# Matmuls on a tile of ones while the first loads run, the first norm's squares from the feature-major x, and first loads on two queues

## The chip, the cores and the metric

The kernel runs on one core of a Trainium2 chip. The metric is the device time of one execution in microseconds (us); the time before the change is the median of three runs. The core has a matrix engine (PE, with its weight loads shown apart as PEld), a vector engine (DVE), an activation engine (ACT), a general engine (POOL) and a queue engine (SP). Each works through its own list of instructions strictly in the order in which the program was built; an instruction that has to wait for another engine holds back everything behind it on its own engine. DMA transfers are issued from SP, ACT or POOL.

## The reference

One layer of a trunk on a sequence of 512 tokens with 1024 features, in float32:

```python
h = rms_norm(x, g[0])                      # x * rsqrt(mean(x^2) + eps) * g
y = hybrid_mixer(h, w_in, ...)             # four branches on proj = h @ w_in, gates on h @ w_gate
x = x + rms_norm(y, g[1])
h = rms_norm(x, g[2]); mem_n = rms_norm(mem, g[4])
x = x + rms_norm(cross_attention(h, mem_n, ...), g[3])
h = rms_norm(x, g[5])
x = x + rms_norm(conv_ffn(h, ...), g[6])
```

The change touches the first line alone, and the part of `proj` with which the kernel begins: the columns v (256, the values of the gated linear attention), a_lr (16, its decay input) and sv (256, the spatial gate's input).

## The kernel before

x is held feature-major, as eight tiles `x[k]` of 128 features by 512 tokens. A float32 product is made of three matmuls on operands split into a high and a low part (`hi`, `lo`): hi·hi, lo·hi and hi·lo. The norm's gain is folded into the split of x (`xgh`, `xgl`, lines 253 and 260), and its factor per token, rs0 = 1/sqrt(mean(x²) + eps), is applied only when a product leaves PSUM. So the matmuls can begin before the norm is known.

The first stage is a loop over the eight feature tiles k (lines 242 to 271). For each k it loads `x[k]` and a 128x528 slice of weights for v, a_lr and sv, splits both on ACT and DVE, and issues 18 matmuls: twelve of 272 columns into four banks `va` (one for each 128 tokens) and six of 256 columns into two banks `sv`. The sums of squares come from a second copy of x, token-major (`x_rows`): `RowNorm.step` loads 128x512 pieces, and ACT squares and sums each along its rows (`row`, lines 205 to 209), eight pieces in all. After the loop rs0 is one square root on ACT (line 194) and one reciprocal on DVE (line 195), and four small matmuls (`bctok`, line 221) spread it over the partitions into `rb0s`, so that it can also be applied to feature-major products.

Then the banks of the first stage are emptied by ACT with the factor rs0 (`svt`, `altok`, `vt`), the second half of the tokens of sv gets its 48 matmuls in the two banks that `svt` frees, `altok` is transposed on PE (`alT`), and the w_in products follow (`win`, 24 matmuls of 512 columns each, in the same two banks, tag A). Beside the first three w_in products runs the decay chain of the gated linear attention: matmuls `z`, then `ee` on ACT, which takes turns with the square root of the spatial gate's layer norm (`sd`, line 371) and with the constants of the recurrence (`la`, line 526), each needing another function table, then scans on DVE (line 421). `kr` (line 352) is the DVE instruction that empties the bank of each of the first two w_in products, and so lets the third and the fourth one start.

What sets the order on each engine is the building scheduler: it takes the instructions by priority and readiness by its own estimate and writes a fixed list for each engine; `with tc.high_priority()` (line 272) moves rs0 and `bctok` ahead as soon as it holds them for ready. The hardware then keeps to that list. SBUF slots (`get`, `put`) are reused in turn, and weights are loaded by SP two or three units ahead into four raw buffers, the same four that the first stage uses.

## Time and profile before

| | us |
|---|---|
| median of three runs (lowest, highest) | 963.23 (962.56, 964.26) |
| the profiled execution, its own time | 964.2 |
| its span in the trace | 960.8 |
| PE busy within the span | 944.7 |
| first matmul of the program, from the span's start | 4.52 |
| first matmul of the first w_in product | 31.97 |
| first matmul of the fourth w_in product | 54.49 |

The span is what the trace covers; 3.4 us of the execution's own time lie around it. Times of single rows are counted from the span's start. In a row of the timeline the first number is the start, the second the time until the end of the last of its instructions (x4 is four of them in a row), and brackets at its end name how long the engine had been idle and what released it. Matmuls are pipelined: the next one starts before the one ahead has ended, so the pace is read from start to start.

### The profile page before, as it was taken

How to read it: one execution, taken by the hardware profiler on the slowest of the kernel's cores; microseconds unless marked ns; L12 is line 12 of the kernel's file. 1: busy time of each engine (PE TensorE's matmuls, PEld its weight loads, DVE VectorE, ACT ScalarE, POOL GpSimd, SP SyncE). 2: the span in 40 equal slices, each digit the busy share in tenths (PEclk: the TensorE clock that was granted, in tenths of full speed). 3: DMA queues.
4: the chain of work that ended last, by engine and by line, in shares of the span. 5: the costliest groups of instructions: out<-in, count | busy, mean ns of one | idle time of the engine just before them, and what ended most of it. 6: DMA issues, size and time to landing. Idle time of an engine off the chain costs nothing.

```text
span 960.8 us, 12143 instructions
## 1 busy us (share of the span) xinstructions
PE 944.7 (98%) x4782; PEld 801.1 (83%) x4782; DVE 575.4 (60%) x886; ACT 420.8 (44%) x637; POOL 11.9 (1%) x33
## 2 busy tenths in 40 slices
PE   8999999999999999999999999999999999999996
PEld 8878887888888888899888899888888888888885
DVE  5876567535454567359854736887767777522414
ACT  7836336423232534356633645644444444322311
POOL 2000000000000000000000000000000000000001
PEclk9999999999999999999999999999999999999998
DMA  9432121232334332435322420232222323233302
GB/s 333 146 112 88 67 91 63 88 99 78 108 113 148 117 105 67 131 111 190 130 75 66 134 86 2 88 109 88 100 98 89 110 88 98 83 104 99 100 1 87
DMA packets 32648, 98.27 MB, mean 102 GB/s; under 512 B 4288, under 2 KB 7248, under 8 KB 32592
## 3 DMA queue, kind: packets, MB, share of 16 engines
q1 hardware_dynamic: 32416, 97.48, 31.2%
q8 instruction: 37, 0.61, 0.3%
q14 instruction: 19, 0.16, 0.0%
q0 software_dynamic: 32, 0.02, 0.0%
q10 hardware_dynamic: 144, 0.00, 0.0%
HBM read 95.39 MB, written 2.10 MB: 101 GB/s over the span
## 4 chain that ended last, share of the span: by engine, by line
PE 93%; DVE 2%; ACT 2%; issue 2%; DMA 0%; DVEq 0%; ACTq 0%
PE up L127 8%; PE up L126 8%; PE up L125 8%; PE gate L126 6%; PE gate L125 6%; PE gate L127 6%; PE dn L125 4%; PE dn L127 4%; PE dn L126 4%; PE win L125 3%; PE win L127 3%; PE win L126 3%; PE wo L125 2%; PE wo L127 2%; PE wo L126 2%
## 5 line engine op out<-in xcount | busy, mean ns | idle before, releaser
L75 ACT CAST whi<-raw 128x1024 fp32r<-128x1024 f32 x158 | 164.4, 1042 | 301.9 <-issue 142.0
L76 DVE TENSOR_TENSOR wlo<-raw,whi 128x1024 fp32r<-128x1024 f32 x158 | 191.3, 1213 | 130.1 <-ACT whi L75 128.8
L127 PE MATMUL up<-h3h,wlo 128*128 128x512 f32 (+1 forms) x368 | 138.2, 376 | 0.0
L126 PE MATMUL up<-h3l,whi 128*128 128x512 f32 (+1 forms) x368 | 138.1, 375 | 0.0
L125 PE MATMUL up<-h3h,whi 128*128 128x512 f32 (+1 forms) x368 | 138.1, 375 | 0.0
L125 PE MATMUL gate<-xgh,whi 128*128 128x512 f32 x256 | 99.8, 390 | 0.0
L126 PE MATMUL gate<-xgl,whi 128*128 128x512 f32 x256 | 99.7, 389 | 0.0
L127 PE MATMUL gate<-xgh,wlo 128*128 128x512 f32 x256 | 99.6, 389 | 0.0
L125 PEld LDWEIGHTS up<-h3h,whi 128*128 128x128 f32 x368 | 69.3, 188 | 12.6
L126 PEld LDWEIGHTS up<-h3l,whi 128*128 128x128 f32 x368 | 69.3, 188 | 12.4
L127 PEld LDWEIGHTS up<-h3h,wlo 128*128 128x128 f32 x368 | 69.3, 188 | 12.4
L352 DVE TENSOR_TENSOR sg<-gate,rb0s 128x512 f32<-128x512 f32 x32 | 22.1, 691 | 79.0 <-PE gate L127 78.9
L544 DVE SCALAR_TENSOR_TENSOR c<-u,par,c 128x511 f32<-128x511 f32 (+1 forms) x88 | 65.0, 746 | 1.3
L125 PE MATMUL dn<-gh,whi 128*128 128x512 f32 x154 | 59.9, 389 | 0.0
L126 PE MATMUL dn<-gl,whi 128*128 128x512 f32 x154 | 59.9, 389 | 0.0
L127 PE MATMUL dn<-gh,wlo 128*128 128x512 f32 x154 | 59.9, 389 | 0.0
L125 PE MATMUL win<-xgh,whi 128*128 128x512 f32 x144 | 57.1, 397 | 1.8 <-DVE la L535 1.8
L125 PEld LDWEIGHTS gate<-xgh,whi 128*128 128x128 f32 x256 | 48.1, 188 | 10.1
L126 PEld LDWEIGHTS gate<-xgl,whi 128*128 128x128 f32 x256 | 48.1, 188 | 9.9
L127 PE MATMUL win<-xgh,wlo 128*128 128x512 f32 x144 | 56.3, 391 | 0.0
L127 PEld LDWEIGHTS gate<-xgh,wlo 128*128 128x128 f32 x256 | 48.1, 188 | 9.9
L126 PE MATMUL win<-xgl,whi 128*128 128x512 f32 x144 | 56.1, 390 | 0.0
(348 smaller groups left out, 1729.9 us busy)
## 6 DMA issues: line engine op xcount, KB each, us to landing
raw<-in_w_up SPq DMA_DIRECT2D x44, 512.0 KB, 3.5
raw<-in_w_gate SPq DMA_DIRECT2D x32, 512.0 KB, 3.5
raw<-in_w_in SPq DMA_DIRECT2D x18, 512.0 KB, 3.6
raw<-in_w_down SPq DMA_DIRECT2D x16, 512.0 KB, 3.6
raw<-in_w_br SPq DMA_DIRECT2D x8, 512.0 KB, 3.4
raw<-in_w_mix SPq DMA_DIRECT2D x8, 512.0 KB, 3.5
raw<-in_w_k SPq DMA_DIRECT2D x8, 512.0 KB, 3.6
raw<-in_w_v SPq DMA_DIRECT2D x8, 512.0 KB, 3.5
```

Of the source, the lines that this page charges most:

```text
L75: scalar.copy(hi[:, :n], raw[:, :n])
L76: vector.tensor_tensor(lo[:, :n], raw[:, :n], hi[:, :n].bitcast(F32), op=ALU.subtract)
L125: tensor.matmul(ps, lhsT=w[0], rhs=x[0], start=first, stop=False)
L126: tensor.matmul(ps, lhsT=w[0], rhs=x[1], start=False, stop=False)
L127: tensor.matmul(ps, lhsT=w[1], rhs=x[0], start=False, stop=last)
L352: vector.tensor_tensor(t, ps, rb0s, op=ALU.mult)
L544: vector.scalar_tensor_tensor(dst[:, s:S], src[:, 0:S - s], pc(wname, (taps - 1 - s) * stride + off), dst[:, s:S], op0=ALU.mult, op1=ALU.add)
```

## The change

- **Spin.** DVE fills a tile with ones, and PE runs seven 128x512 matmuls on it into a bank that nothing reads, ahead of everything else.
- **Squares from the feature-major x.** `x_rows` is no longer loaded. ACT squares each `x[k]` as it stands (`sq`), POOL adds the eight squares into the first (seven 128x512 additions), and rs0 now comes out of `rstd_tok`: four matmuls with a column of ones (`sumtok`) sum over the partitions, then square root and reciprocal as before.
- **First loads on two queues.** The first 272 weight columns and the norm's gains are packed into one array (`w_vg`, 280 columns). ACT's queue issues it, the rest of the weights of k=0, and the weights of k=1; SP's queue issues x[0] in two halves and the other tiles. The high part of x[0] is made in the same two halves. The load of the square root's table (`warm`) stands behind these three issues on ACT.

```diff
--- before.py
+++ after.py
@@ -24,6 +24,7 @@
 EPS = 1e-6
 
 NSLOT = 76
+SPIN = 7
 LOOK = 2
 POOL_OUT = (0, 2, 3, 5)
 
@@ -165,6 +166,13 @@
     def gcol(n, k):
         return pc("norm", n * KT + k)
 
+    idle = bank("C", "idle")
+    spin = get("spin", F32R)
+    vector.memset(spin.bitcast(F32), 1.0)
+    for _ in range(SPIN):
+        tensor.matmul(idle, lhsT=spin[:, 0:P], rhs=spin, start=True, stop=True)
+    put(spin)
+
     ident = cp.tile([P, P], F32, name="ident")
     make_identity(nc, ident)
     ones = cp.tile([P, 1], F32, name="ones")
@@ -172,7 +180,6 @@
     epsc = cp.tile([P, 1], F32, name="epsc")
     gpsimd.memset(epsc, EPS)
     warm = tp.tile([P, 1], F32, tag="warm", bufs=1, name="warm")
-    scalar.activation(warm, ones, AF.Sqrt)
     halfones = cp.tile([P, 2], F32, name="halfones")
     gpsimd.memset(halfones, 0.0)
     gpsimd.memset(halfones[0:64, 0:1], 1.0)
@@ -228,10 +235,10 @@
     VA = 256 + 16
     vps = [bank("B", f"va{t}") for t in range(4)]
     sps = [bank("A", f"sv{t}") for t in range(2)]
-    gn0 = cp.tile([P, KT], F32, name="gn0")
-    scalar.dma_start(gn0, a["par"][:, 0:KT])
+    wg0 = cp.tile([P, VA + KT], F32, name="wg0")
+    gn0 = wg0[:, VA:VA + KT]
     xg, svw = [], []
-    xnorm = RowNorm(a["x_rows"], 4, "rs0")
+    xsum = []
 
     def rows(ps, k, wpair, tiles):
         for i, (xi, wi) in enumerate(((0, 0), (1, 0), (0, 1))):
@@ -240,25 +247,32 @@
                               start=k == 0 and i == 0, stop=k == KT - 1 and i == 2)
 
     for k in range(KT):
-        sync.dma_start(x[k], a["xT"][k])
         raw = wp.tile([P, 1024], F32, tag="raw", bufs=4, name=f"rawv{k}")
         if k == 0:
-            sync.dma_start(raw[:, 0:VA], a["w_vs"][k][:, 0:VA])
-            sync.dma_start(raw[:, VA:VA + 256], a["w_vs"][k][:, VA:VA + 256])
+            scalar.dma_start(wg0, a["w_vg"])
+            sync.dma_start(x[k][:, 0:256], a["xT"][k][:, 0:256])
+            scalar.dma_start(raw[:, VA:VA + 256], a["w_vs"][k][:, VA:VA + 256])
+            sync.dma_start(x[k][:, 256:S], a["xT"][k][:, 256:S])
+            rv = wg0
         else:
-            sync.dma_start(raw[:, 0:VA + 256], a["w_vs"][k])
+            sync.dma_start(x[k], a["xT"][k])
+            (scalar if k == 1 else sync).dma_start(raw[:, 0:VA + 256], a["w_vs"][k])
+            rv = raw
+        if k == 1:
+            scalar.activation(warm, ones, AF.Sqrt)
         if k == 4:
             sync.dma_start(par, a["par"])
         hi, lo = get("xgh", F32R), get("xgl", F32R)
-        scalar.activation(hi, x[k], AF.Copy, scale=gn0[:, k:k + 1])
         wh = wp.tile([P, 1024], F32R, tag="whi", bufs=4, name=f"whv{k}")
         wl = wp.tile([P, 1024], F32R, tag="wlo", bufs=4, name=f"wlv{k}")
+        for c in ((slice(0, 256), slice(256, S)) if k == 0 else (slice(0, S),)):
+            scalar.activation(hi[:, c], x[k][:, c], AF.Copy, scale=gn0[:, k:k + 1])
         if k == 0:
-            vector.tensor_copy(wh[:, 0:VA], raw[:, 0:VA])
+            vector.tensor_copy(wh[:, 0:VA], rv[:, 0:VA])
         else:
-            scalar.copy(wh[:, 0:VA], raw[:, 0:VA])
+            scalar.copy(wh[:, 0:VA], rv[:, 0:VA])
         vector.scalar_tensor_tensor(lo, x[k], gn0[:, k:k + 1], hi.bitcast(F32), op0=ALU.mult, op1=ALU.subtract)
-        vector.tensor_tensor(wl[:, 0:VA], raw[:, 0:VA], wh[:, 0:VA].bitcast(F32), op=ALU.subtract)
+        vector.tensor_tensor(wl[:, 0:VA], rv[:, 0:VA], wh[:, 0:VA].bitcast(F32), op=ALU.subtract)
         xg.append((hi, lo))
         if k % 2 == 0:
             svw.append((get("svwh", F32R), get("svwl", F32R)))
@@ -268,12 +282,18 @@
         vector.tensor_tensor(sl, raw[:, VA:VA + 256], sh.bitcast(F32), op=ALU.subtract)
         rows(vps, k, (wh[:, 0:VA], wl[:, 0:VA]), range(4))
         rows(sps, k, (sh, sl), (0, 1))
-        xnorm.step((0, 0, 1, 1, 1, 1, 2, 2)[k])
+        sq = get("sq")
+        scalar.activation(sq, x[k], AF.Square)
+        xsum.append(sq)
+        if k > 0:
+            gpsimd.tensor_add(xsum[0], xsum[0], sq)
+            put(sq)
     with tc.high_priority():
-        rs0 = xnorm.rstd()
+        rs0 = rstd_tok(xsum[0:1], "rs0")
         rb0 = bcast_tok(rs0)
         rb0s = get("rb0s")
         scalar.copy(rb0s, rb0)
+    put(xsum[0])
     prefetch(3)
 
     vt = [get("vt") for _ in range(2)]
...
     d["w_vs"] = np.concatenate([seg["v"], seg["alr"], seg["sv"]], axis=1).reshape(KT, P, 528)
+    d["w_vg"] = np.concatenate([d["w_vs"][0][:, 0:272], cols(i["norm_g"][0])[:, 0:KT]], axis=1)
```

What the scheduler makes of it, at three places.

**PE, the last two tiles of the first loop.** `sq` is the sum of the eight squares. Before, the broadcast of rs0 stood behind all of the loop's matmuls:

```order
L239 MATMUL va_11_96<-whv_315,xgh_312 128x272
L239 MATMUL va_12_97<-whv_315,xgh_312 128x272
...
L239 MATMUL sv_13_98<-svwl_321,xgh_351 128x256
L239 MATMUL sv_14_99<-svwl_321,xgh_351 128x256
L221 MATMUL bctok_389<-ident,rs_47_386 128x128 x4
L239 MATMUL sv_58_430<-svwh_115,xgh_107 128x256
```

Now (whv_329 belongs to k=6, whv_365 to k=7, the last):

```order
L246 MATMUL va_12_104<-whv_329,xgh_327 128x272
L246 MATMUL va_13_105<-whv_329,xgh_327 128x272
L194 MATMUL sumtok_394<-ones,sq_146 128x1 x4
L246 MATMUL va_14_106<-whv_329,xgh_327 128x272
...
L246 MATMUL sv_15_107<-svwl_336,xgh_327 128x256
L228 MATMUL bctok_402<-ident,rs_50_399 128x128 x4
L246 MATMUL sv_16_108<-svwl_336,xgh_327 128x256
L246 MATMUL va_11_103<-whv_365,xgh_363 128x272
```

The sum over the partitions, which needs the square of the last tile, stands behind the third matmul of k=6; 15 matmuls of k=6 and the 18 of k=7 come after it, and the broadcast stands ahead of the last matmul of k=6.

**POOL, during the first loop.** `st`, `ss`, `scanm` and `causal` are tiles of the gated linear attention that are filled early; `walpha` is a small load. Before:

```order
L329 DMA walpha<-in_w_alpha 16x256
L332 MEMSET scanm_505 128x512
L335 MEMSET causal 128x128
L333 MEMSET scanm_505 128x8
L449 MEMSET st_1011 128x512
L338 MEMSET causal 64x64 x2
L339 AFFINE_SELECT causal<-causal 64x64 x2
L449 MEMSET st_1014 128x512
L456 MEMSET ss_1017 128x512
L456 MEMSET ss_1018 128x512
```

Now (sq_180 is the square of k=1, sq_391 that of k=7):

```order
L289 TENSOR_TENSOR sq_146<-sq_146,sq_180 128x512
L349 DMA walpha<-in_w_alpha 16x256
L289 TENSOR_TENSOR sq_146<-sq_146,sq_216 128x512
L352 MEMSET scanm_518 128x512
...
L289 TENSOR_TENSOR sq_146<-sq_146,sq_250 128x512
L359 AFFINE_SELECT causal<-causal 64x64 x2
L476 MEMSET ss_1030 128x512
L289 TENSOR_TENSOR sq_146<-sq_146,sq_287 128x512
L476 MEMSET ss_1031 128x512
L289 TENSOR_TENSOR sq_146<-sq_146,sq_321 128x512
L289 TENSOR_TENSOR sq_146<-sq_146,sq_357 128x512
L289 TENSOR_TENSOR sq_146<-sq_146,sq_391 128x512
```

The fills that POOL did before the loop's data came now stand between the additions.

**DVE, beside the first w_in products.** `m` and `e` are tiles of the decay chain, `ep` its last factor. Before, `kr` of the first w_in product stood ahead of the chain's end:

```order
L375 TENSOR_TENSOR vn_594<-vn_594,lngb_488 128x256
L352 TENSOR_TENSOR kr_624<-win_528,rb0s_394 128x512
...
L76 TENSOR_TENSOR wlo_631<-raw_629,whi_630 128x1024
L420 TENSOR_TENSOR m_518<-m_518,ee 128x512
L420 TENSOR_TENSOR m_519<-m_519,ee 128x512
L421 SCALAR_TENSOR_TENSOR e_516<-scanm_505,m_518 128x512
```

Now:

```order
L440 TENSOR_TENSOR m_532<-m_532,ee 128x512
L441 SCALAR_TENSOR_TENSOR e_529<-scanm_518,m_531 128x512
...
L445 TENSOR_TENSOR m_532<-e_530 128x512
L450 TENSOR_TENSOR ep_528<-ep_528,rb0s_407 128x512
L372 TENSOR_TENSOR kr_637<-win_541,rb0s_407 128x512
```

The first `kr` now comes behind the scans and both `ep`. On ACT the table loads for `la` and for the later `sd` now stand ahead of the first `ee`, where they stood between the two `ee` and behind them.

## The prediction

> **What bounds the kernel now.** I read the busy time by engine first, then the chain of waits, then what PE waited for.

> ```profile
> PE 944.7 (98%) x4782; PEld 801.1 (83%) x4782; DVE 575.4 (60%) x886; ACT 420.8 (44%) x637; POOL 11.9 (1%) x33
> PE 93%; DVE 2%; ACT 2%; issue 2%; DMA 0%; DVEq 0%; ACTq 0%
> PE va L239 <- ACT xgh L253: 4.5, 1, 4.5
> PE win L125 <- DVE la L535: 1.8, 1, 1.8
> ```

> PE is busy for 944.7 of the span's 960.8 us. The last two rows are its two longest waits: 4.5 us until the first operands are there, and 1.8 us ahead of the fourth w_in product. So I cut the span at those places (columns: stretch, its length, busy time and number of PE, PEld, DVE, ACT and POOL, then granted clock, DMA share, GB/s).

> ```profile
> core 0: us, PE busy (x) PEld busy (x) DVE busy (x) ACT busy (x) POOL busy (x), PEclk, DMA share, GB/s
> 4.52:9.01 4.49, 4.49 (x19) 4.22 (x20) 3.71 (x8) 3.20 (x7) 0.00 (x0) 1.00 1.03 340
> 5.00:24.90 19.90, 19.90 (x146) 19.63 (x146) 11.45 (x26) 15.94 (x40) 3.33 (x8) 1.00 1.04 384
> 31.97:54.49 22.52, 20.76 (x115) 16.34 (x113) 21.07 (x60) 18.48 (x26) 0.52 (x1) 1.00 0.25 88
> 54.49:960.80 906.31, 896.50 (x4466) 757.81 (x4466) 535.90 (x791) 377.23 (x552) 4.72 (x7) 1.00 0.30 96
> 13.84 1.50 PE va L239 x12
> 15.34 0.71 PE sv L239 x6
> 20.48 1.50 PE va L239 x12
> 25.79 2.86 PE sv L239 x24
> ```

> The last four rows are from the chain, with start and length; they give PE's settled pace: a tile k takes 1.50 + 0.71 = 2.21 us (0.125 us for a matmul of 272 columns, 0.119 for one of 256). The first 19 matmuls took 4.49 us instead of about 2.3, although the column of the granted clock shows 1.00: they ran at half pace. From 54.49 on PE is busy for 896.5 of 906.3 us, and there its order is unchanged. So the change is worth what it moves the fourth w_in product's first matmul, at 54.49 now; I work that out.

> **The start.** Now the first matmul waits for the gains (`gn`) and then for `xgh`; the table load on ACT lies before.

> ```profile
> 0.81 0.39 ACTq L232 DMA_DIRECT2D gn<-in_par  x1
> 1.23 1.28 ACT L175 ACT_TABLE_LOAD   x1 [1.23 <-PEq L1054]
> 3.74 0.72 ACT L253 ACTIVATE xgh<-x,gn 128x512 fp32r<-128x512 f32 x1 [1.02 <-DMA gn<-in_par]
> ```

> With the change ACT issues three transfers, 0.39 us or a little more each, from 0.81 to about 2.2; then the table load (1.28) and `warm` (0.2) run to 3.7, the half of `xgh` takes about 0.45 to 4.15. The seven matmuls on ones begin at about 1.3 (after a 0.5 us fill); at half pace 512 columns take 4.49/19 × 512/267 = 0.45 us, so they end at about 4.4. The first real matmul therefore stands at about 4.4 instead of 4.52: 0.1 us won. If half pace lasts some 4.9 us from the first matmul as now (to about 9.4), it ends at 1.3 + 4.9 = 6.2, and 1.8 us of real work at half pace lose 0.9. PE then reaches the fourth matmul of k=6 at 4.4 + 0.9 + 6 × 2.21 + 0.38 = 18.9. Without the change the same place is 20.48 + 0.38, at about 20.8. This 1.9 us is what spin and early loads can bring.

> **The new wait.** At that place PE now stands before `sumtok`, which needs all eight squares added up on POOL. So what counts is when POOL's seventh addition ends; call that T. ACT's rounds first:

> ```profile
> 2.21 0.43 SPq L243 DMA_DIRECT2D x<-in_xT  x1
> 6.04 0.72 ACT L253 ACTIVATE xgh<-x,gn 128x512 fp32r<-128x512 f32 x1 [0.35 <-DMA x<-in_xT]
> 15.31 0.42 ACT L259 CAST whv<-rawv 128x272 fp32r<-128x272 f32 x1
> 15.64 0.40 ACT L267 CAST svwh<-rawv 128x256 fp32r<-128x256 f32 x1
> 15.94 0.63 ACT L208 ACTIVATE row<-row 128x512 f32<-128x512 f32 x1
> 16.58 0.72 ACT L253 ACTIVATE xgh<-x,gn 128x512 fp32r<-128x512 f32 x1
> 17.34 0.42 ACT L259 CAST whv<-rawv 128x272 fp32r<-128x272 f32 x1
> ```

> A round of four operations takes 17.34 − 15.31 = 2.03 us; without the accumulator's read, which the new square doesn't have, about 1.95. x[1] was SP's fourth issue, at 2.21, and there at 6.04, 3.8 us later; as the third, at 0.81 + 2 × 0.47 = 1.74, it is there at about 5.55. The square of k=1 then ends at 5.55 + 0.76 + 0.33 + 0.30 + 0.63 = 7.6, that of k=7 six rounds later, at 19.3. The removed `x_rows` (eight of the pieces that kept the DMA share at 1.04) take no time off this: ACT still squares eight 128x512 tiles. Their cover is the other loads, which at 384 GB/s bring a tile's 0.53 MB in 1.4 us, less than a round.

> Now POOL, from 7.6 on:

> ```profile
> L978 POOL TENSOR_TENSOR out<-x,out 128x256 f32<-128x256 f32 x4 | 3.1, 815 | 868.7 <-DVE out L976 868.7
> L329 POOL DMA_DIRECT2D walpha<-in_w_alpha x1 | 0.6, 643 | 0.0
> L332 POOL MEMSET scanm<- 128x512 f32 x1 | 0.5, 524 | 0.0
> L335 POOL MEMSET causal<- 128x128 f32 x1 | 0.2, 209 | 0.0
> L978 POOL TENSOR_TENSOR out<-x,out x4: 722/815/907, 953.5 to 955.7; 128x256 f32<-128x256 f32 x4
> ```

> The trace has no 128x512 addition on POOL. The two fills give a fixed part of about 0.10 us (0.315 us for 384 columns more); so from 128x256 in 0.722, 0.815 and 0.907 us an addition of 512 columns follows as 1.34, 1.53 and 1.71 us. I take 1.53: these four ran beside DVE additions, and in the first loop DVE also works on two SBUF operands most of the time. Between the additions stand `walpha` (0.64), `scanm` and `causal` (0.52 + 0.21), and the eight `st`, `ss` and `causal` pieces that make up POOL's 3.33 us in the window 5.00:24.90. Its first addition starts at 7.6, and with 7 × 1.53 + 0.64 + 0.73 + 3.33 = 15.4 us of work and no pause (every later square is there first) it ends at T = 23.0. PE stands from 18.9 to 23.0. That the additions go to an engine that is 1% busy hides nothing: this list of POOL is what PE waits for.

> [...]

> **From T to the fourth w_in product.**

> ```profile
> 421.15 1.05 PE L187 MATMUL sumtok<-ones,sq 128*128 128x1 f32 x8
> 422.06 0.36 PE L125 MATMUL kT<-memh,whi 128*128 128x256 f32 x1
> 24.74 1.05 PE L221 MATMUL bctok<-ident,rs 128*128 128x128 f32 x8
> 25.55 0.36 PE L239 MATMUL sv<-svwh,xgh 128*128 128x256 f32 x1
> 29.17 0.47 ACT L287 ACTIVATE altok<-va,rs 128x16 f32<-128x16 f32 x2
> 29.50 1.61 ACT L290 ACTIVATE vt<-va,rs 128x256 f32<-128x256 f32 x4
> 31.97 0.40 PE L125 MATMUL win<-xgh,whi 128*128 128x512 f32 x1
> ```

> `sumtok` holds PE for 0.91 us, nine `va` take 1.13, five `sv` 0.59, `bctok` 0.81 (root and reciprocal fit under the 1.7 us before it), one `sv` 0.12, k=7 2.21: the loop ends at T + 5.77. Now all four `altok`, then one `vt`, then `svt` stand between it and the next `sv`, for which `svt` must free a bank; today a `svt` ran beside the last `sv`. `altok` starts when the last `va` is done, 0.7 before the loop's end: 0.1 + 4 × 0.17 + 0.40 + 0.47 puts the bank free about 0.95 after that end. Then 48 `sv` × 0.119 = 5.72. The first w_in product starts at T + 12.44 = 35.4, against 31.97: 3.5 us later.

> Something comes back in the next stage:

> ```profile
> 34.81 1.28 ACT L526 ACT_TABLE_LOAD   x1
> 36.91 1.28 ACT L371 ACT_TABLE_LOAD   x1
> 38.51 1.28 ACT L417 ACT_TABLE_LOAD   x1
> 39.98 0.68 DVE L352 TENSOR_TENSOR kr<-win,rb0s 128x512 f32<-128x512 f32 x1
> 49.45 0.68 DVE L430 TENSOR_TENSOR ep<-ep,rb0s 128x512 f32<-128x512 f32 x1
> ```

> The first two of these loads now stand before `ee`, under the second half of `sv`, where ACT is free. So the decay chain is 2 × 1.28 + 0.4 = about 3.0 us shorter from the first w_in product on. But the first `kr`, at 39.98 now, moves behind the last `ep`: counted as if the stage began at 31.97 it ends at 49.45 + 0.6 − 3.0 + 0.7 = 47.7, and the third w_in product, which needs its bank, could start at 47.1. It waits 0.65; the fourth no longer does (`kr` two ends at about 51.3). Idle time goes from 22.52 − 20.76 = 1.76 to 0.65: 1.1 us won.

> The sum is T + 12.44 − 31.97 − 1.1 = T − 20.6: for T = 23.0, **2.4 us slower**. Against the profiled execution's 964.2 (span 960.8 and 3.4 around it) that is 966.6; this execution was 1.0 above the median, so for the median 963.23 + 2.4 = 965.6.

> Bounds: additions of 1.34 or 1.71 us move T by 1.3 either way, x[1] half a microsecond earlier or later by 0.5. T from 21.2 to 24.8, sum from +0.6 to +4.2.

> **Rivals.** A difference under 0.2% (1.9 us) is taken for none.

> *PE falls back to half pace while it stands.* The first 19 matmuls show that PE starts slow, the idle 1.76 us before the fourth w_in product that a short pause doesn't bring this back; 4.1 us is longer than any pause in this trace after the start. A new start like the first one would cost 4.49 − 2.3 plus some 0.2 later, 2.4 us: 968.0. [...]

> *POOL keeps up, ACT's last square sets T.* It ends at 19.3, and one addition at the shortest row's 1.34 us behind it gives T = 20.6 and a sum of 0.0: 963.2, no change. It decides if seven additions and the rest of POOL's list fit into the 13 us from 7.6 on, that is below 1.2 us each. For it: POOL's shortest row is 0.722. Against it: even that gives 1.34 us, with which POOL would end at 21.7.

> *PE sets the pace after all.* If data come earlier and squares take less than I read, `sumtok` finds its sum at 18.9: 18.9 − 20.6 = −1.7, 961.5, the start's whole gain. It decides if T is under 19. Against it: the last square alone would have to end at 17.5, nearly two ACT rounds earlier.

> **How the numbers follow.** Forecast 0.48 (slower 0.31, same 0.17, as the middle lies just past the bound), fall-back 0.17 (slower), POOL keeps up 0.22 (same), PE's pace 0.13 (faster 0.09, same 0.04). Slower 0.48, same 0.43, faster 0.09. The range from 962.0 to 968.2 holds the forecast's bounds, POOL keeping up and most of the fall-back.

> **What will show it.** The steps: first `va` near 4.4 and half pace ending near 6; in PE's waits a new row, `sumtok` for POOL's `sq`, of about 4 us; POOL busy without pause from 7.6 to 23, additions near 1.5 us; first `win` at 35.4; only 0.65 us of idle before the third `win`. It is wrong if the additions take 1.1 us or less, if PE hardly waits at `sumtok`, or if matmuls behind it start 0.23 instead of 0.125 us apart, which is the fall-back.

## The result: 970.3 us, 0.76% slower

The change takes 970.3 us in the median of six runs (969.21 to 974.28); the kernel before, run on the same chip, 963.58. The ratio is 1.0076, with a 95% interval of 1.0062 to 1.0091. The direction was forecast, the size was not: 6.7 us are lost instead of 2.4, and 970.3 lies outside the range of 962.0 to 968.2. The profiled execution took 969.98 us, its span 968.3.

The page's busy times and its chain of waits, after:

```profile
PE 951.2 (98%) x4797; PEld 806.3 (83%) x4797; DVE 582.1 (60%) x886; ACT 419.5 (43%) x630; POOL 22.5 (2%) x40
PE 91%; DVE 2%; ACT 2%; issue 2%; POOL 2%; DMA 1%; SPq 0%; DVEq 0%; POOLq 0%; ACTq 0%
```

POOL, absent from the chain before, now holds 2% of it. PE's busy time has grown by 6.5 us; most of this are the 15 added instruction records (the seven matmuls on ones take 3.35 us, the eight passes of `sumtok` 1.87). PE's waits up to 70 us show where POOL's share sits:

```profile
PE sumtok L194 <- POOL sq L289: 3.7, 1, 3.7
PE idle L173 <- DVE spin L171: 1.5, 1, 1.5
PE va L246 <- DVE wlv L275: 0.9, 1, 0.9
PE win L126 <- DVE kr L372: 0.5, 1, 0.5
```

The wait at `sumtok` is the forecast one. What was not forecast as likely stands behind it, in PE's timeline:

```profile
20.71 0.54 PE L246 MATMUL va<-whv,xgh 128*128 128x272 f32 x3
24.99 1.87 PE L194 MATMUL sumtok<-ones,sq 128*128 128x1 f32 x8 [3.74 <-POOL sq L289]
27.09 1.11 PE L246 MATMUL va<-whv,xgl 128*128 128x272 f32 x4
28.00 1.11 PE L246 MATMUL va<-wlv,xgh 128*128 128x272 f32 x4
31.53 0.66 PE L246 MATMUL va<-whv,xgh 128*128 128x272 f32 x4
32.03 0.66 PE L246 MATMUL va<-whv,xgl 128*128 128x272 f32 x4
```

Four `va` take 28.00 − 27.09 = 0.91 us, and from 31.53 on 0.50 again: PE works at half pace in between. Cut at the places where the trace's record of the clock changes, the windows say the same (columns as in the prediction's windows; the granted clock is the third from the end):

```profile
17.45:20.86 3.41, 3.41 (x30) 3.41 (x30) 3.41 (x6) 2.58 (x6) 3.15 (x6) 1.00 0.94 264
20.86:24.27 3.41, 0.39 (x4) 0.17 (x2) 3.41 (x3) 0.72 (x1) 3.25 (x3) 1.00 0.88 249
24.27:27.69 3.42, 2.70 (x12) 2.70 (x13) 2.26 (x3) 0.74 (x2) 0.77 (x2) 0.50 0.59 162
27.69:31.10 3.41, 3.41 (x18) 3.41 (x17) 2.36 (x2) 1.51 (x2) 0.54 (x1) 0.50 0.60 173
```

So the clock was granted at half for 6.83 us, from 24.27 to 31.10. In the trace of before there is no such stretch between the start and the last products.

Because PE's order is the same in both from the w_in products on, the loss can be followed by the start of equal matmuls. The first `win` starts at 40.26 (before 31.97, +8.29), later ones up to the first `gate` about 7.1 later:

```profile
149.42 0.39 PE L125 MATMUL gate<-xgh,whi 128*128 128x512 f32 x1
```

```profile
156.49 0.39 PE L126 MATMUL gate<-xgh,whi 128*128 128x512 f32 x1
```

The first row is of before, the second of after, 7.07 us later (the medians differ by 6.7). The 8.29 us are lost before 41 us, and 1.22 of them come back in the decay stage. In the experiments I use this first `gate` as the mark: its start minus 149.42 is what a run has lost so far.

### The profile page after: what moved, and what is told of

The parts are those of the page before. It is cut to its first block, busy times and chain, and to the rows that moved or that the text cites. A ratio compares the mean times of both kernels' runs of the same rounds, so it can differ in the third digit from the quotient of the medians.

```text
span 968.3 us, 12173 instructions
## 1 busy us (share of the span) xinstructions
PE 951.2 (98%) x4797; PEld 806.3 (83%) x4797; DVE 582.1 (60%) x886; ACT 419.5 (43%) x630; POOL 22.5 (2%) x40
## 4 chain that ended last, share of the span: by engine, by line
PE 91%; DVE 2%; ACT 2%; issue 2%; POOL 2%; DMA 1%; SPq 0%; DVEq 0%; POOLq 0%; ACTq 0%
PE up L128 8%; PE up L127 8%; PE up L126 8%; PE gate L126 6%; PE gate L127 6%; PE gate L128 6%; PE dn L126 4%; PE dn L128 4%; PE dn L127 4%; PE win L126 3%; PE win L127 3%; PE win L128 3%; PE wo L128 2%; PE wo L126 2%; PE wo L127 2%
```

## The experiments

**The theory after seeing the traces.** (1) The squares part carries the loss; spin and the two queues cost or bring little. (2) It loses because POOL's sum is late, for two reasons: POOL's additions are slow, and x[1] comes late. (3) A second price comes from the clock, which falls to half because PE does almost nothing for some 3.4 us (busy for 0.39 of 3.41). **Rivals:** the moved loads and the spin are what makes it slow; the place that the scheduler gave to `sumtok` is; the half pace comes from the tiny products (one column each), not from the pause.

### The change without its squares part

The squares of `x_rows` are put back; spin and the two queues stay.

```diff
-    xsum = []
+    xnorm = RowNorm(a["x_rows"], 4, "rs0")
...
-        sq = get("sq"); scalar.activation(sq, x[k], AF.Square) ... gpsimd.tensor_add(xsum[0], xsum[0], sq)
+        xnorm.step((0, 0, 1, 1, 1, 1, 2, 2)[k])
...
-        rs0 = rstd_tok(xsum[0:1], "rs0")
+        rs0 = xnorm.rstd()
```

> The change without its middle part: matmuls on ones and first loads on two queues stay, the sums of squares come from the token-major x again, as before. Theory (spin and early loads bring at most the 1.9 us by which PE reaches k=6 earlier, and the squares alone cost the loss): no wait for POOL, the broadcast as before near the loop's end; PE reaches the loop's end 1 to 2 us before the kernel before, time 961.5 to 963.5. Rival (the spin or the two queues carry a part of the loss): above 965.

Measured: 963.04 us, ratio 1.0002 (0.999 to 1.0014); mark at +0.17 (three of the ten runs, at a mean clock of 0.993 to 0.995, took 965.6 to 966.3). Spin and queues together are neutral, the squares part carries the loss. PE's waits show why the earlier start brings nothing:

```profile
PE va L246 <- ACT whv L273: 1.2, 1, 1.2
PE bctok L228 <- DVE rs L202: 0.4, 1, 0.4
```

PE is at full clock from 5.1 us, but waits for the data of k=1 and later for rs.

### The squares part alone, on the kernel before

```diff
-    xnorm = RowNorm(a["x_rows"], 4, "rs0")
+    xsum = []
...
-        xnorm.step((0, 0, 1, 1, 1, 1, 2, 2)[k])
+        sq = get("sq")
+        scalar.activation(sq, x[k], AF.Square)
+        xsum.append(sq)
+        if k > 0:
+            gpsimd.tensor_add(xsum[0], xsum[0], sq)
+            put(sq)
...
-        rs0 = xnorm.rstd()
+        rs0 = rstd_tok(xsum[0:1], "rs0")
```

> The kernel before with the squares alone: no products on ones, first loads as before, POOL adds the squares. Theory (the squares carry the loss, and the moved loads add 1.6 us to it by bringing x[1] at 7.15 instead of 5.55): first addition at about 7.7, last one ends at 23.0 to 23.5, PE waits 2 to 3 us at `sumtok`; first `win` at 35.5 to 36.0 and 966.0 to 967.0 us if the clock holds, 2.9 us more if it falls back. Rival (the moved loads and the products on ones are what makes the sums late): no wait at `sumtok` over 1 us, 963 to 964 us.

Measured: 971.34 us, ratio 1.0074 (1.0051 to 1.0097), and single runs from 966.7 to 972.5. The profiled one, the fastest, has its mark at +3.72:

```profile
7.83 1.29 POOL L275 TENSOR_TENSOR sq<-sq,sq 128x512 f32<-128x512 f32 x1 [5.74 <-ACT sq L272]
22.84 1.31 PE L187 MATMUL sumtok<-ones,sq 128*128 128x1 f32 x8 [2.05 <-POOL sq L275]
```

With the loads as before the first addition starts at 7.83 (7.6 was the prediction's figure for the change) and the sum is there at 22.8. The change's own first addition starts at 9.18, and its sum is there at 24.94. So without the moved loads (and the spin) the first addition starts 1.35 us earlier and the sum comes 2.15 earlier, and POOL's list alone makes it late anyway. The clock falls back here too, for 3.41 us from 23.49. The other three runs have a mean clock of 0.989 to 0.991 against 0.995 in this one, so they were at half pace for longer; where, no trace shows.

### DVE adds instead of POOL

```diff
-            gpsimd.tensor_add(xsum[0], xsum[0], sq)
+            vector.tensor_add(xsum[0], xsum[0], sq)
```

> The change with the seven additions on DVE in place of POOL, order and all else the same. Theory (POOL's pace, and how POOL and DVE slow each other, make the sums late): an addition takes about 0.65 us, no split of DVE is stretched over 0.8 us, last addition ends at 22.5 to 23.5, wait at `sumtok` 1 to 2.3 us, first `win` at 35.0 to 36.0 and 965.5 to 966.8 us if the clock holds, to 969.5 us if it falls back. Rival (the squares themselves come late, whichever engine adds): last addition at 24.5 or later, 969 to 971 us.

Measured: 964.76 us, ratio 1.001 (0.9997 to 1.0022), better than either theory said; mark at +0.61. The trace, of a run at a mean clock of 0.997, shows no half pace between the start and the last products; three of the ten runs, at 0.993, took 966.8 to 967.0.

```profile
L289 DVE TENSOR_TENSOR sq<-sq,sq x7: 672/674/686, 9.5 to 21.3; 128x512 f32<-128x512 f32 x7
22.13 1.02 PE L194 MATMUL sumtok<-ones,sq 128*128 128x1 f32 x8 [0.54 <-DVE sq L289]
33.79 0.40 PE L126 MATMUL win<-xgh,whi 128*128 128x512 f32 x1
```

One addition takes 0.674 us on DVE. On POOL, in the change:

```profile
L289 POOL TENSOR_TENSOR sq<-sq,sq 128x512 f32<-128x512 f32 x7 | 10.8, 1543 | 7.4 <-ACT sq L286 7.1
14.34 2.56 POOL L289 TENSOR_TENSOR sq<-sq,sq 128x512 f32<-128x512 f32 x1
15.66 1.78 DVE L274 SCALAR_TENSOR_TENSOR xgl<-x,wg,xgh 128x512 fp32r<-128x512 f32 x1
18.61 1.42 POOL L289 TENSOR_TENSOR sq<-sq,sq 128x512 f32<-128x512 f32 x1
18.13 0.74 DVE L274 SCALAR_TENSOR_TENSOR xgl<-x,wg,xgh 128x512 fp32r<-128x512 f32 x1
18.80 1.54 DVE L275 TENSOR_TENSOR wlv<-rawv,whv 128x272 fp32r<-128x272 f32 x1
```

1.54 us in the mean (the rows above are the group of additions, then single rows of POOL's and DVE's timelines). Beside an addition DVE's splits take 1.78 and 1.54 us instead of 0.74 and 0.43; with DVE adding, all eight `xgl` take 0.73 to 0.75 and all `wlv` at most 0.48. So the two engines hold each other up here, where both read two operands; beside POOL's fills, which read none, and its AFFINE_SELECT, which reads one, the splits nearly keep their time (0.74 us for the `xgl` of 12.96, 0.47 for the `wlv` of 17.36). Why, no run shows; the ends of the rows show how: they take turns. The `xgl` that starts at 15.66 ends at 17.44, 0.55 us after the addition that ends at 16.89; the `wlv` of 18.80 ends 0.30 after the addition of 18.61. In the traces of the change, of the squares alone and of the next run, each of the seven additions holds up one split, and all 21 of these splits end 0.28 to 0.31 us (256 or 272 columns) or 0.55 to 0.56 us (512 columns) after it. The 2.56 us are the same the other way round: that addition ends 1.16 us after the third of three splits in a row, at 15.74. In the change the seven held-up splits are 7.3 us longer together than their undisturbed likes.

This one word of the source is worth 970.3 − 964.8 = 5.5 us. Not all else stayed the same with it, though the order of the program did: the scheduler now puts `sumtok` eleven matmuls later into PE's list (behind fourteen of k=6 instead of three), which is 1.36 us of PE's work. No run separates that part.

### POOL's early fills and `walpha` ahead of the loop

```diff
+    walpha = cp.tile([16, 256], F32, name="walpha")
+    gpsimd.dma_start(walpha, a["w_alpha"])
+    scanm = get("scanm") ... causal = cp.tile(...) ... early = [get("st") for _ in range(2)] + [get("ss") for _ in range(2)]
...
     for k in range(KT):
```

> The change, with POOL's early fills (scan mask, causal mask, four zeroed tiles of the linear attention) and the small load written ahead of the first loop, so that POOL does them before its first addition instead of between the additions. Sums over the partitions stay inside k=6. Theory (POOL's list sets the wait, and 4 us of it are those fills): additions follow each other with at most a wait for the next square, the last ends at 21.3 to 22 us (the last square ends at 19.97 in the change) instead of 24.95, PE waits below 1.2 us, no half pace, first w_in product at about 34, time 963.5 to 965. Rival (the additions themselves, slowed by DVE, set it): the last addition still ends after 23.5 and the time stays above 967.

Measured: 968.92 us, ratio 1.0054 (1.0034 to 1.0074). The sum is there at 22.0, 3.0 earlier than in the change, and PE no longer waits at `sumtok`; first `win` at 37.20, 3.06 earlier than in the change, and mark at +4.08:

```profile
16.04 0.77 PE L262 MATMUL va<-wlv,xgh 128*128 128x272 f32 x4 [0.70 <-DVE wlv L291]
22.64 0.54 PE L262 MATMUL va<-whv,xgh 128*128 128x272 f32 x3
23.02 0.95 PE L194 MATMUL sumtok<-ones,sq 128*128 128x1 f32 x8
```

But the profiled run took 970.47, since it lost some 2.5 us more far from the start (windows at the `o` products of the gated linear attention's second pair):

```profile
158.57:161.98 3.41, 3.41 (x28) 2.61 (x26) 3.25 (x8) 1.09 (x2) 0.00 (x0) 1.00 0.25 97
161.98:165.39 3.41, 2.84 (x20) 2.31 (x17) 3.15 (x10) 0.76 (x2) 0.00 (x0) 1.00 0.00 0
165.39:168.80 3.41, 3.41 (x14) 2.97 (x12) 1.74 (x2) 3.36 (x4) 0.00 (x0) 0.50 0.35 114
168.80:172.21 3.41, 3.41 (x9) 2.71 (x9) 0.63 (x2) 0.51 (x2) 0.00 (x0) 0.50 0.10 40
```

Half pace from 165.39 on, for 6.83 us, behind a window in which PE is busy for 2.84 of 3.41 us. Two of its runs without it (mean clock 0.996 and 0.997) took 967.92 and 968.04. So, first, 4.4 us are lost without any half pace and without a wait at `sumtok`. What the first `win` gains here on the change is little more than the half pace that is missing (2.7 us, worked out at the end): now PE itself is late. Its first `va` of k=6, at 22.64, stood at 20.71 in the change and at 20.48 before; it has waited twice 0.70 us for `wlv`, whose splits on DVE the additions hold up (1.54 and 1.55 us instead of 0.43), and behind `sumtok` it waits 1.3 us more (0.53 for rs, 0.35 for `altok`, 0.45 for `svt`). So the wait at `sumtok` is only the form that the loss takes in the change, and the theory's point (2) is not enough. And second, the half pace isn't bound to the long wait.

### Matmuls in the pause

Three versions fill part or all of the wait with fp32 products of the last square, ahead of `sumtok`: eight of 128 columns (against `ident`), or seven or four of 512, as here.

```diff
     with tc.high_priority():
+        for _ in range(FILL):
+            tensor.matmul(idle, lhsT=sq[:, 0:P], rhs=sq, start=True, stop=True)
         rs0 = rstd_tok(xsum[0:1], "rs0")
```

Eight of 128 columns:

> The change, with eight more 128x128 float32 matmuls on PE, on the square of k=7, ahead of the sums over the partitions; nothing reads them, and nothing else is changed but that the sums now stand three matmuls earlier. They keep PE busy for about 1.8 us of the 3.7 us wait; POOL's last addition still ends at about 25. Theory (PE falls back to half pace because it stands still for more than 3.4 us): the pause is below 3.2 us, matmuls behind the sums start 0.125 us apart, first w_in product at about 38, time 967 to 968. Rival (the half pace behind the wait has another cause, POOL or DVE traffic or the float32 sums themselves): matmuls of 272 columns still start 0.227 us apart, time 970 to 971.

Measured: 969.98 us, ratio 1.0064 (1.0039 to 1.0088). `sumtok` itself now runs at full pace, but the clock falls back one window later:

```profile
24.09:27.50 3.41, 1.96 (x16) 1.96 (x17) 3.41 (x4) 1.11 (x2) 1.34 (x1) 1.00 0.78 221
27.50:30.91 3.41, 3.41 (x18) 3.41 (x17) 1.85 (x3) 1.33 (x2) 0.63 (x1) 0.50 0.60 180
```

One run whose mean clock was 0.997, with no room for such a stretch, took 968.35. Seven of 512 columns:

> The change, with seven extra fp32 products of 512 columns ahead of the first `sumtok`; they read the last square (there at about 20.0 us) and go to the unused `idle` bank, so PE works through most of the time in which it now waits for POOL. Nothing else is different, the sums still come at about 25.0. Theory (the wait at `sumtok` makes the clock fall to half for 6.8 us, and that costs 2.9 us beside the wait itself): no half-pace stretch after 25, products behind `sumtok` 0.125 apart, first `win` at about 37.4 to 38.0 where the change has 40.26, 967.0 to 967.8 us. Rival (the half pace comes from the tiny products or from something else at that place): the stretch stays, first `win` at 40, 969.5 to 970.5 us.

Measured: 970.29 us, ratio 1.0074 (1.0058 to 1.009). I had taken a product for half its cost: it is two passes of 0.43 us.

```profile
21.48 6.17 PE L294 MATMUL idle<-sq 128*128 128x512 f32 x14
27.49 0.95 PE L195 MATMUL sumtok<-ones,sq 128*128 128x1 f32 x8
29.16 1.13 PE L229 MATMUL bctok<-ident,rs 128*128 128x128 f32 x8
```

`sumtok` starts 2.50 later than in the change, yet the first `win` (40.56) only 0.30 later: the clock stays at 1.00 throughout, from 6.9 to 962.7 us (of its four runs one has a mean clock of 0.995, the others 0.996 or 0.997). The tiny products are all there, so they alone are not what lowers the clock. The time showed nothing, as the overlong fill took what the clock gave. Four of 512 columns:

> The change with four in place of seven extra fp32 products of 512 columns ahead of the first `sumtok` (each takes two passes, 0.44 us an half, 0.88 us the product in the run with seven, so PE is busy with them from about 21.5 to 25.0, as long as POOL needs). Theory (the half pace costs what the wait leaves behind, and comes only if a stretch of 3.4 us has almost no columns in it): `sumtok` at 25.0 to 25.2, no half pace, first `win` at 38.0 to 38.3 (the run with seven: 40.56 less 2.4), 967.6 to 968.2 us. Rival (the long fill of the run with seven held the clock up only because it lasted 6 us): half pace again, first `win` near 40, 969.5 to 970.5 us.

Measured: 970.16 us, ratio 1.0068 (1.005 to 1.0085); two runs at a mean clock of 0.997 took 969.05 and 969.06, the profiled one, at 0.992, 972.03. My "no half pace" was wrong for this one (first `win` at 42.12):

```profile
23.83:27.24 3.41, 2.28 (x15) 1.56 (x13) 3.41 (x4) 0.58 (x2) 1.26 (x2) 1.00 0.64 183
27.24:30.65 3.41, 2.77 (x13) 2.81 (x14) 0.49 (x2) 0.59 (x1) 0.90 (x1) 0.50 0.74 257
```

PE is busy for 2.28 of the 3.41 us ahead of the drop, and its waits there are short (0.8 us at `sumtok`, 0.95 at `bctok`). What the stretch lacks is columns (1,352).

### What lowers the clock

In all traces the half-clock stretches between the start and the last products last 3.41 or 6.83 us, and the full-clock ones between are whole multiples of 3.413 (17.07, 20.48, 153.60, 160.43, 931.84 us are 5, 6, 45, 47 and 273). So in these traces the clock changes only at the steps of a grid of 3.413 us. I counted, for each window of that grid, the columns of all matmul passes that start in it (a 512-column product in the kernel's three-pass form counts 3 × 512); back to back, at 0.227 us for 512, a window holds some 7,700. Over thirteen traces, windows at full clock:

| columns in a window | next window | where |
|---|---|---|
| 128 to 2168, nineteen windows | half clock, all nineteen | change 20.86 (272); squares alone 20.08 (1078); four fills 23.83 (1352); fills first 161.97 (1920); cast on DVE 157.23 (2048); eight small fills 24.09 (2168); the other thirteen at the end of the program, one in each trace |
| 2304, 2368 | full | eight small fills 164.03; change 164.22 |
| 2360 | half | in order, 24.37 |
| 2752 and more, all others | full | before's lowest: 156.3 (3712) |

In these traces the border is near 2,300 columns, 30% of a full window, with a few per cent of doubt since some records may be missing. Idle time explains it badly: a window with PE busy for 2.84 of 3.41 us dropped the clock, one of the run with the cast on DVE with PE busy for only 1.66 us (51.41, 3072 columns) didn't. The border was drawn afterwards, on the same traces from which it is read. The small products of the second `o` stage give 1,920 to 3,712 columns in their thinnest window depending on where the grid lies over them; that is a second place at which these kernels may lose some 2 us (2.5 in the run with the fills first, 1.8 in the one with the cast on DVE). Before, with 3,712 in its one trace, may do so too: among its runs beside the experiments are one of 967.9 us at a mean clock of 0.993 and one of 966.1 at 0.995; where they lost it no trace shows.

### The sum in its plain place

Without `high_priority` all loop products come first and `sumtok`, `bctok` behind them.

```diff
-    with tc.high_priority():
-        rs0 = rstd_tok(xsum[0:1], "rs0")
-        rb0 = bcast_tok(rs0)
...
+    rs0 = rstd_tok(xsum[0:1], "rs0")
+    rb0 = bcast_tok(rs0)
```

> The change, with the norm's factor without priority: the scheduler puts the sums over the partitions and the broadcast behind all 144 matmuls of the first loop, as the broadcast stood before. POOL's list is unchanged. Theory (the wait inside the loop and PE's slow restart make the loss): PE runs k=6 and k=7 through until about 25.1 us, which is when POOL's last addition ends (24.95 in the change), so no wait above 0.5 us before the sums and no half pace behind them; the loop's end, the sums, root, reciprocal and broadcast then follow one another, first w_in product at about 34, against 40.26 in the change and 31.97 before; time 964 to 965. Rival (the loss comes from POOL and DVE sharing memory access, or from later data, wherever the sums stand): the additions are all there, so the time stays at 969 to 971.

Measured: 968.69 to 971.98 us in four runs, ratio 1.0066 (1.0046 to 1.0087); the theory's 964 to 965 was wrong. A fifth, profiled execution took 5.1 ms, for reasons that its trace doesn't show, and isn't used; the kernel was run again for a trace:

> The change with the first norm's `sumtok` and `bctok` behind all products of the loop over k, once more, for its trace. In its earlier runs 968.7 to 972.0 us at a mean granted clock of 0.989 to 0.993. Theory: PE doesn't wait at `sumtok` (the loop ends at about 25, as do the sums), yet waits over 1 us for rs ahead of `bctok`, with tiny products around it, and so falls to half pace there; without that it would be 965.5 to 966.5 us. Rival (the half pace in these runs comes far from the start, in the small products on `ss` at about 160): the stretch lies at 155 to 175, and first `win` at 36.5 to 37.5.

Measured: 968.80 us, ratio 1.0052 (1.0036 to 1.0068), mark at +5.98. PE's timeline, then ACT's and DVE's:

```profile
26.10 0.95 PE L194 MATMUL sumtok<-ones,sq 128*128 128x1 f32 x8
29.78 2.05 PE L228 MATMUL bctok<-ident,rs 128*128 128x128 f32 x8 [2.73 <-DVE rs L202]
```

```profile
26.78 1.04 ACT L76 CAST whi<-raw 128x1024 fp32r<-128x1024 f32 x1 [1.75 <-DMA raw<-in_w_in]
27.73 0.26 ACT L201 ACTIVATE rs<-sumtok,epsc 128x4 f32<-128x4 f32 x1
25.63 3.92 DVE L77 TENSOR_TENSOR wlo<-raw,whi 128x1024 fp32r<-128x1024 f32 x3
```

No wait at `sumtok`, but one of 2.73 at `bctok`: on ACT the square root stands behind the cast of a weight unit that lands only at 26.8, and on DVE the reciprocal, which starts at 29.47, stands behind three splits of weight units. The clock falls to half from 27.79 on. So moving `sumtok` out of the loop doesn't remove the pause, it moves along; what that place would cost without any wait, no run shows.

### The spin alone, and a cast moved

On the kernel before: the seven matmuls on ones alone, then with the cast to `svwh` moved as well.

```diff
+    idle = bank("C", "idle")
+    spin = get("spin", F32R)
+    vector.memset(spin.bitcast(F32), 1.0)
+    for _ in range(SPIN):
+        tensor.matmul(idle, lhsT=spin[:, 0:P], rhs=spin, start=True, stop=True)
+    put(spin)
```

> The kernel before with the seven products on ones alone. Theory: PE is at full pace from about 5 us instead of 9.5, so the products of k=1 start about 1.5 us earlier (7.3), but `bctok` still waits for the norm's own chain on ACT, ready at about 24.2, so that of the 1.5 to 1.8 us no more than 0.5 to 1.0 are left at the first `win` (31.0 to 31.5, before 31.97): 962.4 to 963.2 us. Rival (the early products bring all they save): first `win` at 30.2, 961.7 us. Rival (they bring nothing, as with the loads on two queues): 963.4 to 963.8 us.

Measured: 962.34 us, ratio 0.999 (0.9977 to 1.0002), first `win` at 31.69, only 0.28 earlier. PE is at full clock from 5.6 instead of 9.5 us; it waits instead further on:

```profile
20.21 0.63 ACT L216 ACTIVATE row<-row 128x512 f32<-128x512 f32 x1 [1.32 <-DMA row<-in_x_rows]
22.11 0.76 PE L247 MATMUL va<-whv,xgh 128*128 128x272 f32 x4 [1.06 <-ACT whv L267]
```

ACT stands 1.32 us for a piece of `x_rows`, and the split of k=7 behind it makes PE wait 1.06.

```diff
-        scalar.copy(sh, raw[:, VA:VA + 256])
+        vector.tensor_copy(sh, raw[:, VA:VA + 256])
```

> The kernel before with the seven products on ones, and with the cast to `svwh` moved from ACT (0.40 us for each of the eight k) to DVE, which has time there. Theory (ACT's chain to the first norm is what holds the start once the clock is up): the chain is up to 2 us shorter, `bctok` no longer waits, first `win` at 30.0 to 30.8, 961.6 to 962.4 us. Rival (PE's own products, or the loads, set the pace): as the products on ones alone, 962.4 to 963.2 us.

Measured: 962.22 us, ratio 0.999 (0.9981 to 0.9999), no different from the spin alone (first `win` 31.62), so this cast on ACT is not what held the start. The profiled run fell to half for one window at 160.64, behind 2,048 columns.

### Spin, and columns in the thin stretch

This is the spin alone with three more products. If the border above is real, three spare products in the second pair's `o` stage, where PE waits three times 0.19 us for DVE, must end the runs that the spin alone had at 963.7 to 965.5.

```diff
+        fillo = bank("C", "fillo") if p == 1 else None
         for n in range(1, 8):
+            if p == 1 and n > 4:
+                tensor.matmul(fillo[:, 0:192], lhsT=st[0][:, 0:P], rhs=st[1][:, 0:192], start=True, stop=True)
             tensor.matmul(o_ps[:, n * 64:(n + 1) * 64], ...
```

> The kernel before with the seven products on ones, and three spare products of 192 columns (fp32, into a bank that nobody reads) ahead of the last three products on `ss` of the second GLA pair, where PE waits 0.19 us each for DVE. Three of eleven runs with the products on ones alone were 963.7 to 965.5 us at a mean clock of 0.993 to 0.995. Theory (those runs fall to half pace in the stretch of small products at 157 to 161, when a 3.4 us stretch of the clock happens to lie over it): no run over 963.2 us, all at 0.996 or 0.997, median 961.9 to 962.5 us. Rival (the slow ones fall back elsewhere): 2 to 4 of 11 runs stay at 963.7 to 965.6 us.

Measured: 962.39 us, ratio 0.9986 (0.9977 to 0.9995), all eleven runs between 961.65 and 963.02 at a mean clock of 0.996 to 0.998. The window that holds the stage:

```profile
157.74:161.15 3.41, 3.41 (x23) 2.92 (x23) 3.19 (x9) 1.82 (x2) 0.00 (x0) 1.00 0.00 0
```

PE is busy in all of it, with some 4,300 columns. This is the one run that was forecast from the count of columns, and it came out as forecast. It doesn't part columns from idleness, as the spare products also take up the waits for DVE; and if a run of the spin alone takes 963.7 us or more in 3 of 11 cases, eleven without any such come by chance in about 3% of cases (8/11 to the eleventh power), where the 3 of 11 is itself a rough figure. It beats both given kernels, the one before by 1.2 us. Against the spin alone (962.34) the median is the same; what is gone are the runs of 963.7 to 965.5 us at a mean clock of 0.993 to 0.995.

## Why the prediction was right and wrong

Two steps of the prediction failed: the time T at which POOL's sum is there, which hung on x[1] at 5.55 us, and the half pace, which stood beside the sum as a rival instead of in it. With T alone put right the prediction's own sum gives 24.99 − 20.6 = 4.4, or 967.6 us; the half pace carries it to 970.3.

**Right: what PE would wait for.** The new wait at `sumtok` for POOL's seventh addition is there, 3.7 us long (4.1 forecast). That POOL's additions are the cause is shown by the run with DVE adding, in which nearly all of the loss is gone. The additions take 1.54 us in the mean (1.53 taken), POOL's list from first addition to last is 15.8 us long (15.4). The mean was in part luck: it is 1.28 when nothing holds the addition up and up to 2.56 when splits on DVE do. The rival *POOL keeps up*, which needed less than 1.2 us, is out: in no trace did POOL add 512 columns faster than 1.27.

**Missing: what the additions do to DVE.** The prediction let POOL's additions be slowed by DVE, but not DVE's splits by POOL (7.3 us over seven splits in the change). There this is largely hidden behind the wait; with POOL's fills moved ahead it shows, as PE came to `sumtok` only at 23.02 though the sum was there at 22.0, and 4.4 us stayed lost.

**Wrong: x[1] at 5.55, so T = 23.0.** T was 24.99. The chain:

```profile
1.73 5.40 DMA x<-in_xT
7.15 0.72 ACT xgh L269
8.49 0.54 ACT sq L286
9.18 1.33 POOL sq L289
```

I let x[1] fly the 3.8 us that it took before. With six transfers started by two queues within the first 2.2 us it took 5.4. That is 1.6 of the 2.0 us; POOL's list gives the other 0.4. The other traces agree, with scatter: in the eight traces of kernels with two queues x[1] takes 5.3 to 6.3 us and lands at 7.1 to 8.0, in the five with one 3.8 to 4.9 and 6.0 to 7.1. Whether the second queue does it or the larger amount that is in flight at once, no run separates. This also removed the gain of the start: half pace ended at 7.2 and the first `va` stood at 4.68 (forecast 6.2 and 4.4), but PE reached the place of `sumtok` at 21.25, not at 18.9. It is also why *PE sets the pace* never came near; with the spin alone, PE's early clock brought 0.28 us at the first `win`, where spin and early loads together were to bring 1.9.

**Right but for a size: T + 12.44.** At full pace, from the run with seven fills: from `sumtok` at 27.49 to the first `win` at 40.56 are 13.07 us, with three `va` and one `sv` more behind it than in the change (0.49), so 12.58.

**Wrong: half pace as a rival with 17%.** The change took 15.27 us for that way, 2.69 more. The price (2.4) was near; the chance was not, and no run showed what it rested on. In the traces the window ahead of a half-pace stretch is not idle, it holds fewer than some 2,300 columns (PE busy for 0.36 to 2.84 of 3.41 us); the wait of 3.7 us left one of 272 columns in the change, and each of its six runs has a mean clock of 0.989 to 0.995 against before's usual 0.997, so the half pace came nearly always. The trace of before, too, shows a way back to half pace, at its end:

```profile
951.61:955.02 3.41, 0.73 (x5) 0.52 (x4) 2.26 (x7) 0.31 (x2) 1.53 (x2) 1.00 0.00 0
955.02:958.43 3.41, 0.00 (x0) 0.00 (x0) 2.35 (x7) 0.00 (x0) 1.61 (x3) 0.50 0.72 238
```

The clock is at half from 955.02 on, behind a window in which PE was still busy for 0.73 us: no whole idle window was needed.

**Right: what comes back.** 8.29 us at the first `win` are 7.07 later on, so 1.22 (1.1 forecast), with one wait of 0.48 before the third `win` (0.65).

The sum redone: 2.4 + 2.0 (T) + 0.14 (the way) + 2.69 (half pace) − 0.12 (given back more) = 7.1, the 7.07 that the trace shows; the way and the half pace are told apart by the run with seven fills, so by another kernel's trace. Without the half pace it is 4.4, so about 968.0 us by the medians; the run at full clock with eight small fills (968.35), whose sum is late as well, lies near.

What stays open: how the 5.5 us of the run with DVE adding divide between the earlier sum, the undisturbed splits, the later place of `sumtok` and the clock; why runs of one kernel differ by one window of half pace or two, beyond the place where the grid happens to lie, and what decides between 2,304 and 2,368 columns.

## What to carry to other kernels

An engine that is 2% busy can still be the one that is waited for (POOL here, for 3.7 us): price the list that a moved reduction queues behind, and don't put two-operand work on POOL beside two-operand work on DVE, as each held the other up here (a split took 1.78 instead of 0.74 us, an addition up to 2.56 instead of 1.28). Where PE's work thins out, count the columns over 3.4 us, not the idle time: the clock fell here behind each 3.41 us window with 2168 columns or fewer, two of them with PE busy for 2.84 us, and the half pace cost 2.7 us in the change. Enough spare columns kept the clock up in the traces of two kernels (seven products of 512 at `sumtok`, three of 192 at the second `o`), too few did not in two others, and with each of the fills at `sumtok` the median stayed within 0.4 us of the change's. Compare single runs by their mean granted clock before arguing over two microseconds.
